# A two-layer streaming encoder on one core: decay tiles and attention tiles put in one ring of seven, a fifth key tile, and a planner reseeded every 16 jobs

## The chip, the core and the metric

The kernel runs on one core of a Trainium2 chip. Five engines work side by side and meet at semaphores: TensorE (PE in the rows of the profile, and PEld for its weight loads), VectorE (DVE), ScalarE (ACT), GpSimd (POOL) and SyncE (SP), which issues every DMA of this kernel. The metric is the device time of one execution in microseconds (us), as the median of repeated runs.

## The reference

The input is one sequence of 2048 frames of width 1024, and two layers act on it. Each computes `x + gate * Mixer(RMSNorm(x) * (1 + scale) + shift)`, where shift, scale and gate are linear in SiLU of a conditioning vector. The first mixer is a gated linear recurrence (RG-LRU). The second is gated DeltaNet with 8 heads of width 128, and the change is made there. For a chunk of frames with summed log-decays `g` it computes

```
decay_mask = exp(where(causal, g[i] - g[j], -inf))
a_mat = where(strict, (k_beta @ k.T) * decay_mask, 0)
t_mat = inverse(a_mat + I)
attn  = where(causal, (q @ k.T) * decay_mask, 0)
v_new = u - w @ state;   o = q_dec @ state + attn @ v_new
state = state * e_last + k_dec.T @ v_new
```

The state is handed from chunk to chunk, so this part is a chain. A final RMSNorm ends the program. All of it is in float32.

## The kernel before

The frames are cut into two units of 1024 (`u`), each into two tiles of 512 (`i`). Layer 1 makes x and z panels of its input projection (`in1`, jobs of 24 matmuls of 128x512, L711), convolves, gates and scans them, and multiplies by its output weights (`out1`). Layer 2 does the same with panels k, v, q and z of each head (`in2`), runs the delta rule per head, and multiplies by its output weights (`out2`). Every projection is three matmuls for a float32 product: high by high, high by low, low by high.

In layer 2 a job's result goes through a convolution (`xe`, `xf`: ACT L1021, then three taps on DVE, L763) and SiLU on ACT (L1028) and becomes `kt`, `qt` or `vt`. For every head and tile of 512 frames, `key_thread` takes a decay tile `ec`: a DMA brings the log-decays, POOL masks them, ACT takes exp of four 128x128 parts (L1139), DVE scales them (L1172). It transposes `kt` on PE (`pk`, L1146) into the token-major keys `kd`, squares these (L1157), and makes `ac`, the strict matrix times decay (L1184). `norm_q_thread` writes the queries to DRAM, reloads them transposed (`pq`) and squares them on ACT (`junkq`, L1219). `query_thread` multiplies q by k on PE (`pqk`, L1268), and DVE multiplies that by `ec` into a tile of its own, `at` (L1273); then `ec` is given back. `inverses_thread` inverts 32x32 blocks on DVE (L1303, L1306). `levels_thread` builds the inverse of 128x128 from these (`px`, `pr`, with `tf` as working tile: L1338 to L1388). `recurrence_thread` runs eight steps per head and unit: `pp` on PE (L1421, L1422), `zt` on DVE (L1430), `py` on PE (L1438), `yt` on ACT (L1444), `pS` on PE (L1450, L1451), the state on DVE (L1463). `decay_thread` makes the decays of a unit from the projection `pab` (L1066), whose split weights (`wabh`, L1052) lie in a `tf` tile until the last `pab`.

ACT has one table of functions at a time. A row `ACT_TABLE_LOAD` stands where the function it needs next (SiLU, exp, sqrt) is in another table.

The order of the instructions on every engine is not written out. A planner, `Weave`, runs while the program is built: each thread is a generator that yields an engine and an assumed duration, a ring of tiles (`Slots`), or an event, and the planner starts next whatever can start first by its own clock; instructions are emitted in that order. So a ring's size, a wait or an assumed duration moves instructions everywhere. Assumed durations off PE are scattered by 1% with a seeded generator, so the seed is also an input to the order. `job()` runs one panel by one tile: 64 jobs in `in1`, 128 in `in2`, 32 in `out1` and 33 in `out2`.

Of the kernel before, what the change touches and what calls it, by code (L numbers as in the profile page):

```python
# [32 lines left out]
KTN, QTN = 6, 5  # L33
MARGIN = 1.0
# [6 lines left out]
SEED, SPREAD = 3, 0.01  # L41
# [34 lines left out]
class Weave:  # L76
    def __init__(self):
        self.free = dict.fromkeys(("pe", "act", "dve", "pool", "sp", "dma"), 0.0)
        self.held = {"dve2": [], "pool2": []}
        self.table = "exp"  # L80
        self.landed, self.through = [0.0] * 8, 0.0
        self.scatter = random.Random(SEED)
        self.threads = []
        self.now = 0.0

# [85 lines left out]
def trunk_kernel(ctx, tc, x, head, small, ada0, ada_w, ada_b, final_g, w1, gate_w, ow1, w2, wab, ow2, out):  # L171
# [44 lines left out]
    def part_of(tile_in, at, *shape):  # L216
# [27 lines left out]
        "xe": 2, "xf": 2, "kt": KTN, "qt": QTN, "vt": 1, "ec": 3, "gr": 1, "middle": 1, "ac": 4, "atn": 4, "kd": 4, "vn": 4,  # L244
        "rq": 4, "nk": 4, "oo": 2, "tblk": 1, "ttmp": 1, "tf": 2, "zt": 2, "t2": 2, "yt": 2, "so": 2, "ro": 2,
# [3 lines left out]
    for t in ("xe", "xf", "vt", "ec", "gr", "middle", "ab", "gin", "gg", "spe", "spd"):  # L249
        tags[t] = ("l2a", tags[t][1])  # L250
    tags |= {"g2": ("o2a", 1), "fg": ("o2a", 1), "xta": ("o2a", 2)}
    tags |= {"oh": ("o2", 3), "ol": ("o2", 3), "xt": ("o2", 4), "ot": ("o2", 2)}
    slots = {t: Slots(n) for t, (_, n) in tags.items()}
    slots["turn"] = Slots(TURN)
    pools.update(xp=xp, ps=ps)
# [487 lines left out]
    def project_thread():  # L743
        for name, panels, jobs in plans:
            if name == ("out1",):
                yield from out1_jobs()
                continue
            for n in range(len(jobs)):
                if name == ("in1", 0) and n < 4:

                    w.spawn(job(name, jobs, n), 8 + n)
                    if n == 3:
                        for m in range(4):
                            yield ev("job", name, m)
                else:
                    yield from job(name, jobs, n)
        yield from out2_jobs()
# [199 lines left out]
    def out1_jobs():  # L957
        nb = S // P
        jobs = [(b + q, d) for b in range(0, nb, 2) for d in range(2) for q in range(2)]
        for b, d in jobs:  # L960
            yh, yl, htok, ltok = yield ev("yhl", b)
            ow = yield ev("owtiles", 1, d)
            bank = "d" if d else "mm"
            mtok = yield slots[bank]
            pt = ps.tile([P, TC], F32, tag=bank, name="mmo")
            yield from products(pt, (yh, yl), ow, (lambda k: ev("ow", 1, d, k // 2 * 2)))
            if d == 1:
                put("yh", htok)
                put("yl", ltok)
            w.spawn(residual1_thread(b, d, pt, bank, mtok), 3, 0.2)  # L970
            if b == nb - 1:
                w.set(ev("free", "out1", d))
# [152 lines left out]
    def key_thread(u, h, i):  # L1125
# [5 lines left out]
        ec = tile_([P, TB, P], "ec", "ec")  # L1131
# [129 lines left out]
    def query_thread(u, h, i):  # L1261
# [8 lines left out]
        xtok = yield slots["atn"]  # L1270
        yield "dve", 0.61
        at = tile_([P, TB, P], "atn", "at")
        dve.tensor_tensor(at, pqk, ec, ALU.mult)  # L1273
        put("tp", ptok)
        put("ec", etok)
        vn, ntk = yield ev("vn", u, h, i)
        toks = {"kt": ktok, "qt": qtok, "ac": atok, "atn": xtok, "kd": dtok, "vn": ntk}
        w.set(ev("parts", u, h, i), (kt, qt, ac, at, kd, vn, toks))
# [117 lines left out]
    def recurrence_thread(u, h):  # L1396
# [4 lines left out]
        for i in range(NTC):  # L1401
# [7 lines left out]
            for b in range(TB):  # L1409
# [45 lines left out]
                if b == TB - 1:  # L1455
                    release(toks, "ac", "vn", "kd", "atn")
# [81 lines left out]
    def queries_end_thread():  # L1538
        for i in range(NTC):
            yield ev("parts", NU - 1, NH - 1, i)  # L1540
            yield ev("rq", NU - 1, NH - 1, i)
        early.close()
# [60 lines left out]
    def out2_jobs():  # L1603
# [4 lines left out]
        for b, q in jobs:  # L1608
            c0, n = parts[b][q]
# [29 lines left out]
    def finish_thread(b, parts):  # L1639
        xt, tag, tok = yield ev("xt", b)  # L1640
        otag = "raw" if b < AHEAD else "ot"
        otok = yield slots[otag]
# [9 lines left out]
        for q in range(1, parts):  # L1652
# [4 lines left out]
        yield "pool", 1.34  # L1657
        rs = tile_([P, 1], "rs", "rs")
        rsqrt(rs, ss[:, 0:1], 1.0 / D, 1)
# [136 lines left out]
```

## Time and profile before

| what | value |
|---|---|
| median of the runs | 1860.39 us (3 runs, 1857.08 to 1862.02) |
| the profiled execution's own time | 1852.99 us |
| its span, first to last instruction | 1851.3 us |
| PE busy | 1798.8 us, 97% of the span |
| DVE, ACT, POOL busy | 1344.0, 1167.0, 358.4 us (73%, 63%, 19%) |
| layer 1 with its output | about 0 to 645 us |
| layer 2, unit 0 and unit 1 | about 645 to 1160 and 1160 to 1690 us |
| second output and final norm | about 1690 to 1851 us |

A row of waits reads: engine and the first instruction after the wait, then what ended the wait, then us in total, how often, and the longest. A row of a timeline reads: start, duration, engine, line, operation, output and inputs, how many, and in brackets the idle time of the engine before it and what ended it. A row of the chain of waits has start, duration and what the chain went through. Matmul ends are modelled, so a busy PE is not a PE at its best rate.

### The profile page before, as it was taken

Reading aid. Unit: us, or ns where it says so; the run is one execution under the profiler, and the core shown is the slowest. Engines: PE = TensorE matmul, PEld = TensorE weight load, DVE = VectorE, ACT = ScalarE, POOL = GpSimd, SP = SyncE. Lnnn points to the kernel's source line nnn. Section 1 sums busy time; section 2 is a strip of 40 time slices with the busy share of each in tenths; the row PEclk is TensorE's granted clock in tenths of the full one; section 3 lists DMA queues with packets and bytes.
Section 4 is the critical chain, followed back from the end, with each engine's and each line's share of the span. In section 5 each row is a group of like instructions: output and inputs, shape, how many; then the busy total and the mean of one; then the engine's idle time right before and its main releaser. Section 6 shows DMA issues by size and latency. Waiting matters only on the chain.

```text
span 1851.3 us, 31018 instructions
## 1 busy us (share of the span) xinstructions
PE 1798.8 (97%) x10270; PEld 1441.3 (78%) x10270; DVE 1344.0 (73%) x3112; ACT 1167.0 (63%) x2709; POOL 358.4 (19%) x896
## 2 busy tenths in 40 slices
PE   6999999999999999999999999999999999999998
PEld 4777777777878877787888787787788877778886
DVE  7989887877455647777888878577776687776653
ACT  5766777666111467786888766777778678654221
POOL 2111001010000013232323221232223223211100
PEclk9999999999999999999999999999999999999999
DMA  9577655545588645567677666366655556687741
GB/s 357 146 205 210 238 190 179 184 156 165 191 217 222 188 126 141 142 167 182 165 165 195 155 162 191 106 162 151 150 141 138 145 142 162 151 224 208 245 144 67
DMA packets 510425, 322.75 MB, mean 174 GB/s; under 512 B 369844, under 2 KB 437940, under 8 KB 510264
## 3 DMA queue, kind: packets, MB, share of 16 engines
q1 hardware_dynamic: 510264, 320.77, 62.0%
q8 instruction: 81, 1.33, 0.3%
q14 instruction: 80, 0.66, 0.1%
HBM read 219.93 MB, written 100.73 MB: 173 GB/s over the span
## 4 chain that ended last, share of the span: by engine, by line
PE 71%; DVE 9%; DMA 7%; ACT 7%; SPq 4%; issue 2%; POOL 1%; DVEq 0%; POOLq 0%; ACTq 0%
PE mm L711 39%; PE mmo L711 18%; PE pg L843 3%; DVE xf L763 2%; DMA raw<-in_w 2%; PE py L1438 1%; PE pp L1421 1%; PE pS L1450 1%; PE pS L1451 1%; PE pp L1422 1%; DVE ttmp L1303 1%; DVE tblk L1306 1%; DMA blk<-blk_d 1%; PE pqk L1268 1%; PE pkk L1180 1%
## 5 line engine op out<-in xcount | busy, mean ns | idle before, releaser
L763 DVE SCALAR_TENSOR_TENSOR xf<-xe,small_s,xf 128x512 f32<-128x512 f32 x288 | 214.1, 749 | 40.8 <-ACT xf L1021 37.2
L687 ACT CAST whi<-raw 128x1024 fp32r<-128x1024 f32 x96 | 100.0, 1042 | 50.1 <-DMA raw<-in_w 43.7
L1303 DVE TENSOR_TENSOR ttmp<-blk,tblk 128x60 f32<-128x60 f32 (+24 forms) x496 | 105.5, 213 | 17.3 <-DMA blk<-blk_d 5.7
L1306 DVE TENSOR_TENSOR tblk<-tblk,ttmp 128x60 f32<-128x60 f32 (+24 forms) x496 | 107.4, 217 | 12.2
L711 PE MATMUL mm<-hh_('in2', 0)_5148,whi 128*128 128x512 f32 x256 | 103.9, 406 | 2.2 <-DVE tf L1350 2.2
L711 PE MATMUL mm<-hh_('in2', 1)_11583,whi 128*128 128x512 f32 x256 | 104.5, 408 | 0.7 <-ACT tz L1036 0.7
L711 PE MATMUL mm<-hh_('in2', 0)_5148,wlo 128*128 128x512 f32 x256 | 104.2, 407 | 0.0
L711 PE MATMUL mm<-hh_('in2', 1)_11803,wlo 128*128 128x512 f32 x256 | 104.1, 407 | 0.0
L711 PE MATMUL mm<-hl_('in2', 1)_11584,whi 128*128 128x512 f32 x256 | 104.0, 406 | 0.0
L711 PE MATMUL mm<-hh_('in2', 1)_11583,wlo 128*128 128x512 f32 x256 | 104.0, 406 | 0.0
L711 PE MATMUL mm<-hl_('in2', 0)_5149,whi 128*128 128x512 f32 x256 | 103.8, 406 | 0.0
L711 PE MATMUL mm<-hl_('in2', 0)_5034,whi 128*128 128x512 f32 x256 | 103.6, 405 | 0.0
L711 PE MATMUL mm<-hl_('in2', 1)_11804,whi 128*128 128x512 f32 x256 | 103.5, 404 | 0.0
L711 PE MATMUL mm<-hh_('in2', 1)_11803,whi 128*128 128x512 f32 x256 | 103.5, 404 | 0.0
L711 PE MATMUL mm<-hh_('in2', 0)_5033,wlo 128*128 128x512 f32 x256 | 103.1, 403 | 0.0
L711 PE MATMUL mmo<-oh,oh 128*128 128x512 f32 (+1 forms) x264 | 102.8, 389 | 0.0
L711 PE MATMUL mmo<-ol,oh 128*128 128x512 f32 (+1 forms) x264 | 102.7, 389 | 0.0
L711 PE MATMUL mm<-hh_('in2', 0)_5033,whi 128*128 128x512 f32 x256 | 102.5, 400 | 0.0
L711 PE MATMUL mmo<-oh,ol 128*128 128x512 f32 (+1 forms) x264 | 102.4, 388 | 0.0
L711 PE MATMUL mmo<-oh,yl 128*128 128x512 f32 x256 | 100.5, 393 | 0.5 <-DVE yl L953 0.5
L711 PE MATMUL mmo<-oh,yh 128*128 128x512 f32 x256 | 100.8, 394 | 0.0
L711 PE MATMUL mmo<-ol,yh 128*128 128x512 f32 x256 | 100.8, 394 | 0.0
(317 smaller groups left out, 5322.0 us busy)
## 6 DMA issues: line engine op xcount, KB each, us to landing
raw<-in_w SPq DMA_DIRECT2D x96, 512.0 KB, 4.2
araw<-in_ada_w SPq DMA_DIRECT2D x32, 512.0 KB, 4.3
xt<-x_d SPq DMA_DIRECT2D x32, 512.0 KB, 5.4
xt_d<-xb SPq DMA_DIRECT2D x192, 64.0 KB, 2.7
xk<-xt_d SPq DMA_DIRECT2D x24, 512.0 KB, 5.7
xt<-in_x SPq DMA_DIRECT2D x16, 512.0 KB, 6.0
ada<-in_ada SPq DMA_DIRECT2D x16, 512.0 KB, 10.4
y_d<-tz SPq DMA_DIRECT2D x32, 256.0 KB, 3.0
```

The costliest lines, as they stand in the source:

```text
L687: act.copy(hi, raw)
L711: pe.matmul(pt, lhsT=lhs[a][:, k, :], rhs=rhs[b][:, k, :], start=(k == 0 and n == 0), stop=(k == KT - 1 and n == 2))
L763: dve.scalar_tensor_tensor(xf, xe[:, 1 + j:1 + j + TC], wc[:, j:j + 1], xf, ALU.mult, ALU.add)
L843: pe.matmul(pg, lhsT=gw[:, g, :], rhs=xf, start=True, stop=True)
L1180: pe.matmul(pkk[:, b, :], lhsT=kc, rhs=kc, start=True, stop=True)
L1268: pe.matmul(pqk[:, b, :], lhsT=kt[:, b * P:(b + 1) * P], rhs=qt[:, b * P:(b + 1) * P], start=True, stop=True)
L1303: dve.tensor_tensor(tmp, blk[:, j, j + 1:32].unsqueeze(2).to_broadcast([P, r, c_]), t[:, j, 0:c_].unsqueeze(1).to_broadcast([P, r, c_]), A ...
L1306: dve.tensor_tensor(t[:, j + 1:32, 0:c_], t[:, j + 1:32, 0:c_], tmp, ALU.subtract)
L1421: pe.matmul(pp[:, 0, :], lhsT=kc, rhs=S_, start=True, stop=True)
L1422: pe.matmul(pp[:, 1, :], lhsT=qc, rhs=S_, start=True, stop=True)
L1438: pe.matmul(py, lhsT=rm[:, b, :], rhs=zt, start=True, stop=True)
L1450: pe.matmul(pS[:, 0, :], lhsT=kd[:, b, :], rhs=yt, start=True, stop=True)
```

## The change

Seven tiles replace three of `ec` and four of `at`: `query_thread` now writes attention over the decays, in place, and the tile is given back when the recurrence has used it. Of the seven, three lie in the part of memory that is closed before the end of layer 2, four in the other; `queries_end_thread` waits for the three. `kd` has five tiles, not four, and `tf` one, not two. The planner's generator is seeded anew each 16 jobs, from a list of 17 seeds. In the last norm, `finish_thread` takes its output tile only after the second output weights were issued, and for the last block of frames it scales two parts of the sum of squares ahead, adds the third on DVE, and takes the power on POOL.

```diff
+EC = 7
-SEED, SPREAD = 3, 0.01
+SEEDS, SPREAD = (32, 45, 51, 36, 4, 54, 53, 16, 3, 25, 36, 8, 28, 14, 37, 0, 0), 0.01
...
+    def count(self):
+        self.jobs += 1
+        if self.jobs % 16 == 0:
+            self.scatter = random.Random(SEEDS[self.jobs // 16])
...
-        "xe": 2, "xf": 2, "kt": KTN, "qt": QTN, "vt": 1, "ec": 3, "gr": 1, "middle": 1, "ac": 4, "atn": 4, "kd": 4, "vn": 4,
-        "rq": 4, "nk": 4, "oo": 2, "tblk": 1, "ttmp": 1, "tf": 2, "zt": 2, "t2": 2, "yt": 2, "so": 2, "ro": 2,
+        "xe": 2, "xf": 2, "kt": KTN, "qt": QTN, "vt": 1, "ec": 4, "eca": 3, "gr": 1, "middle": 1, "ac": 4, "kd": 5, "vn": 4,
+        "rq": 4, "nk": 4, "oo": 2, "tblk": 1, "ttmp": 1, "tf": 1, "zt": 2, "t2": 2, "yt": 2, "so": 2, "ro": 2,
...
+    ECLAST = NU * NH * NTC - 1
+    slots["ec"] = Slots(EC)
...
-        ec = tile_([P, TB, P], "ec", "ec")
+        ec = tile_([P, TB, P], "eca" if (ECLAST - etok) % EC >= 4 else "ec", "ec")
...
-        xtok = yield slots["atn"]
         yield "dve", 0.61
-        at = tile_([P, TB, P], "atn", "at")
-        dve.tensor_tensor(at, pqk, ec, ALU.mult)
+        dve.tensor_tensor(ec, pqk, ec, ALU.mult)
         put("tp", ptok)
-        put("ec", etok)
...
-                    release(toks, "ac", "vn", "kd", "atn")
+                    release(toks, "ac", "vn", "kd", "ec")
+                    w.set(ev("ecfree", toks["ec"]))
...
+        for n in range(4, EC):
+            yield ev("ecfree", ECLAST - n)
...
+        if b < AHEAD:
+            yield ev("owissue", 2, 1)
...
-        for q in range(1, parts):
+        for q in range(1, 2):
...
-        yield "pool", 1.34
-        rsqrt(rs, ss[:, 0:1], 1.0 / D, 1)
+        if parts > 2:
+            yield "pool", 0.28
+            pool.tensor_scalar(ss[:, 0:1], ss[:, 0:1], 1.0 / D, EPS, ALU.mult, ALU.add)
+            yield ev("sq", b, 2)
+            yield "dve", 0.16
+            dve.scalar_tensor_tensor(ss[:, 0:1], ss[:, 2:3], 1.0 / D, ss[:, 0:1], ALU.mult, ALU.add)
+            yield "pool", 0.6
+            pool.tensor_tensor(rs, ss[:, 0:1], mhalf[:, 0:1], ALU.pow)
+        else:
+            yield "pool", 1.34
+            rsqrt(rs, ss[:, 0:1], 1.0 / D, 1)
```

The engines run nearly the same instructions as before: PE has 8350 matmuls in both, SP the same DMAs, DVE one instruction more and POOL one less (the last norm), and ACT has 97 table loads where it had 123. What differs besides is the order. Line numbers are up to 22 higher after the change, so L1038 there is L1028 here.

**First place**, ACT near the start of layer 2: the last `kt` row is the second key tile of head 1, and `junkq` squares the reloaded queries of head 0's second tile. Before:

```order
L775 COPY xe<-mm 128x512
L1157 ACTIVATE junk,ssk<-kd 128x128 x2
L1021 ACTIVATE xf<-xe,small_s 128x512
L1219 ACTIVATE junkq,ssq<-pq 128x128 x3
L1139 ACT_TABLE_LOAD
L1139 ACTIVATE ec<-ec,gc 128x128
L687 CAST whi<-raw_5931 128x1024
L1139 ACTIVATE ec<-ec,gc 128x128 x6
L1219 ACTIVATE junkq,ssq<-pq 128x128
L1139 ACTIVATE ec<-ec,gc 128x128
L1028 ACT_TABLE_LOAD
L1028 ACTIVATE kt<-xf 128x512
```

The same place now:

```order
L1031 ACTIVATE xf<-xe,small_s 128x512
L1167 ACTIVATE junk,ssk<-kd 128x128
L1038 ACTIVATE kt<-xf 128x512
L695 CAST whi<-raw_5935 128x1024
L1149 ACT_TABLE_LOAD
L1149 ACTIVATE ec<-ec,gc 128x128
L1160 COPY kd<-pk 128x512
```

The key tile comes ahead of the exps and both table loads, and `junkq` of that tile follows ten rows behind the last row shown.

**Second place**, DVE, the levels of head 2 in unit 0: `tf<-ac` transposes blocks for the matmuls `px`, and `tf<-px` takes their result back, for `pr` on PE. `tb<-qt` is the transpose of a query tile on its way to DRAM. Before:

```order
L763 SCALAR_TENSOR_TENSOR xf<-xe,small_s,xf 128x512 x6
L1338 STREAM_TRANSPOSE tf<-ac 32x4x32 x2
L1273 TENSOR_TENSOR at<-pqk,ec 128x512
L1338 STREAM_TRANSPOSE tf<-ac 32x4x32 x4
L1234 STREAM_TRANSPOSE tb<-qt 128x512
L693 TENSOR_TENSOR wlo<-raw_7954,whi 128x1024
L1350 TENSOR_SCALAR tf<-px 32x8x32
```

The same place now:

```order
L1345 STREAM_TRANSPOSE tf<-ac 32x4x32
L701 TENSOR_TENSOR wlo<-raw_7838,whi 128x1024
L1345 STREAM_TRANSPOSE tf<-ac 32x4x32
L772 SCALAR_TENSOR_TENSOR xf<-xe,small_s,xf 128x512 x3
L1357 TENSOR_SCALAR tf<-px 32x8x32
L507 TENSOR_SCALAR xt<-xt,rs 128x1024
L1244 STREAM_TRANSPOSE tb<-vt 128x512
```

Three taps stand between the last transpose and `tf<-px`, where a transpose to DRAM and a weight split stood.

**Third place**, DVE where unit 1 begins: `beta` is made from the last `pab`, and the `tf` rows are the levels of head 7 of unit 0. Before:

```order
L1350 TENSOR_SCALAR tf<-px 32x8x32
L613 TENSOR_TENSOR hl_('in2', 1)_11804<-h,hh_('in2', 1)_11803 128x512
L763 SCALAR_TENSOR_TENSOR xf<-xe,small_s,xf 128x512 x2
L1366 COPY ac<-pr 32x4x32
L763 SCALAR_TENSOR_TENSOR xf<-xe,small_s,xf 128x512
L1366 COPY ac<-pr 32x4x32 x2
L1234 STREAM_TRANSPOSE tb<-vt 128x512
L1376 TENSOR_SCALAR tf<-px_12148 64x256
L1385 COPY ac<-pr_12173 64x4x64
L1461 COPY state_106<-pS 128x128
L1471 COPY oo<-pS 128x128
L1087 TENSOR_SCALAR beta<-beta 128x64
```

The same place now:

```order
L1345 STREAM_TRANSPOSE tf<-ac 32x4x32 x4
L1097 TENSOR_SCALAR beta<-beta 128x64
L1345 STREAM_TRANSPOSE tf<-ac 32x4x32
L1101 TENSOR_TENSOR gin<-ab,small_s 128x64
L295 TENSOR_SCALAR gg<-gin 128x64
```

The levels of head 7 were done before `beta`; they begin now only when the last `pab` has let go of the one `tf` tile.

More of the change, by code (lines that the diff above doesn't have):

```diff
@@ L81, in __init__ @@
         self.landed, self.through = [0.0] * 8, 0.0
-        self.scatter = random.Random(SEED)
+        self.scatter, self.jobs = random.Random(SEEDS[0]), 0
         self.threads = []
         self.now = 0.0
+    def count(self):
+        self.jobs += 1
+        if self.jobs % 16 == 0:
+            self.scatter = random.Random(SEEDS[self.jobs // 16])
     def spawn(self, gen, prio, delay=0.0):
@@ L243, in trunk_kernel @@
     tags |= {t: ("l2", n) for t, n in {
-        "xe": 2, "xf": 2, "kt": KTN, "qt": QTN, "vt": 1, "ec": 3, "gr": 1, "middle": 1, "ac": 4, "atn": 4, "kd": 4, "vn": 4,
-        "rq": 4, "nk": 4, "oo": 2, "tblk": 1, "ttmp": 1, "tf": 2, "zt": 2, "t2": 2, "yt": 2, "so": 2, "ro": 2,
+        "xe": 2, "xf": 2, "kt": KTN, "qt": QTN, "vt": 1, "ec": 4, "eca": 3, "gr": 1, "middle": 1, "ac": 4, "kd": 5, "vn": 4,
+        "rq": 4, "nk": 4, "oo": 2, "tblk": 1, "ttmp": 1, "tf": 1, "zt": 2, "t2": 2, "yt": 2, "so": 2, "ro": 2,
         "ssk": 2, "ssq": 2, "rk": 2, "cc": 2, "junk": 1, "ab": 1, "gin": 1, "gg": 1, "spe": 1, "spd": 1, "beta": 2,
         "gs": 2, "eg": 2}.items()}
-    for t in ("xe", "xf", "vt", "ec", "gr", "middle", "ab", "gin", "gg", "spe", "spd"):
+    for t in ("xe", "xf", "vt", "eca", "gr", "middle", "ab", "gin", "gg", "spe", "spd"):
         tags[t] = ("l2a", tags[t][1])
@@ L748, in project_thread @@
             for n in range(len(jobs)):
+                w.count()
                 if name == ("in1", 0) and n < 4:
@@ L960, in out1_jobs @@
         for b, d in jobs:
+            w.count()
             yh, yl, htok, ltok = yield ev("yhl", b)
@@ L1269, in query_thread @@
                       start=True, stop=True)
-        xtok = yield slots["atn"]
         yield "dve", 0.61
-        at = tile_([P, TB, P], "atn", "at")
-        dve.tensor_tensor(at, pqk, ec, ALU.mult)
+        dve.tensor_tensor(ec, pqk, ec, ALU.mult)
         put("tp", ptok)
-        put("ec", etok)
         vn, ntk = yield ev("vn", u, h, i)
-        toks = {"kt": ktok, "qt": qtok, "ac": atok, "atn": xtok, "kd": dtok, "vn": ntk}
-        w.set(ev("parts", u, h, i), (kt, qt, ac, at, kd, vn, toks))
+        toks = {"kt": ktok, "qt": qtok, "ac": atok, "ec": etok, "kd": dtok, "vn": ntk}
+        w.set(ev("parts", u, h, i), (kt, qt, ac, ec, kd, vn, toks))
     def inverses_thread(u, h):
@@ L1608, in out2_jobs @@
         for b, q in jobs:
+            w.count()
             c0, n = parts[b][q]
```

## The prediction

> **What bounds the kernel now.** I read the page's busy line first, then the stretches, the waits of PE, and the chain of waits.
>
> ```profile
> PE 1798.8 (97%) x10270; PEld 1441.3 (78%) x10270; DVE 1344.0 (73%) x3112; ACT 1167.0 (63%) x2709; POOL 358.4 (19%) x896
> 0.00:645.00 645.00, 626.45 (x2689) 485.41 (x2690) 482.85 (x819) 355.63 (x486) 71.21 (x132) 1.00 0.66 204
> 645.00:1160.00 515.00, 501.05 (x3343) 406.96 (x3343) 398.47 (x1106) 381.16 (x1043) 136.92 (x362) 0.99 0.64 161
> 1160.00:1690.00 530.00, 517.70 (x3545) 422.44 (x3544) 376.30 (x1088) 392.37 (x1097) 133.14 (x353) 1.00 0.60 154
> ```
>
> The first row is the page's, the others are stretches (start and end, length, then busy time and count of PE, PEld, DVE, ACT, POOL, granted clock, DMA share and rate). PE bounds the kernel in every stretch, at a granted clock of 0.99 to 1.00. The change leaves PE's 8350 matmuls as they were, so it can gain only where PE stands still: 515.00 - 501.05 + 530.00 - 517.70 = 26.3 us idle in layer 2, plus weight loads that come late. ACT is busy for 381.16 of 515 us there, so it bounds nothing on the average; it matters by what it makes late. PE's waits, with those of its weight loads below (in total, how often, longest):
>
> ```profile
> PE pk L1146 <- ACT kt L1028: 4.2, 4, 3.1
> PE pS L1450 <- ACT yt L1444: 3.8, 5, 1.4
> PE mm L711 <- DVE tf L1350: 2.2, 1, 2.2
> PE py L1438 <- DVE zt L1430: 1.9, 2, 1.4
> PE pp L1421 <- DVE state L1463: 1.8, 3, 0.8
> ...
> PEld py L1438 <- DVE zt L1430: 13.7, 57, 1.9
> PEld pp L1421 <- DVE state L1463: 11.6, 47, 1.3
> PEld pS L1450 <- ACT yt L1444: 9.6, 20, 1.9
> ```
>
> Two single waits stand out, 3.1 us for a key tile and 2.2 us for `tf`. The rest is spread over many short ones, most of them at the recurrence.
>
> **First term, the key tile: -3.0 us.** ACT and PE around the longest wait:
>
> ```profile
> 706.12 0.71 ACT L1021 ACTIVATE xf<-xe,small_s 128x512 f32<-128x512 f32 x1
> 711.27 0.31 ACT L1219 ACTIVATE junkq<-pq 128x128 bf16<-128x128 f32 x1 [4.45 <-DMA pq<-q_d]
> 712.57 1.28 ACT L1139 ACT_TABLE_LOAD   x1
> 713.86 0.40 ACT L1139 ACTIVATE ec<-ec,gc 128x128 f32<-128x128 f32 x1
> 717.57 1.28 ACT L1028 ACT_TABLE_LOAD   x1
> 718.86 0.63 ACT L1028 ACTIVATE kt<-xf 128x512 f32<-128x512 f32 x1
> 719.54 0.33 PE L1146 MATMUL pk<-ident,kt 128*128 128x128 f32 x1 [3.05 <-ACT kt L1028]
> ```
>
> ACT stands for 4.45 us before `junkq`, whose reload is late, then changes tables, runs exps, changes back, and only then makes `kt`. In the new order (first place above) this `kt` comes ahead of the exps, both loads and `junkq`. So I take the whole 3.05 us as gone. If the reload is late again, what stands behind `junkq` now is exps and `kd` rows of head 1, which PE needs only for that head's levels and recurrence, after DVE has inverted its blocks. I cost that at nothing; without this cover the 3 us come back. Bounds: 0 (another row takes its part) to -3.3 (with a late weight load, an estimate).
>
> **Second term, `tf` of head 2: -2.2 us.**
>
> ```profile
> 863.83 0.71 DVE L1234 STREAM_TRANSPOSE tb<-qt 128x512 f32<-128x512 f32 x1 [3.76 <-DMA v_d<-tb]
> 864.46 1.21 DVE L693 TENSOR_TENSOR wlo<-raw,whi 128x1024 fp32r<-128x1024 f32 x1
> 865.70 0.43 DVE L1350 TENSOR_SCALAR tf<-px 32x256 f32<-32x256 f32 x1
> 866.18 0.50 PE L711 MATMUL mm<-hh_('in2', 0)_5148,whi 128*128 128x512 f32 x1 [2.22 <-DVE tf L1350]
> ```
>
> DVE stands for 3.76 us before `tb<-qt`, since a DMA has not yet emptied the tile it writes; behind it wait a weight split and `tf<-px`, and behind that PE. Now three taps stand in that place (second place above), 3 x 0.75 us, that hang on no DMA just before. I counted all 16 levels in the orders: between the last transpose and `tf<-px` stood 13 transposes to DRAM and weight splits, and now 7. So the pattern is rarer, not only gone here. Bounds 0 to -2.2.
>
> **Third term, the table loads: -3.8 us.** The page's groups and the first and last of the table loads on the chain of waits of layer 2:
>
> ```profile
> L1139 ACT ACT_TABLE_LOAD x29 | 37.2, 1283 | 0.5
> L1028 ACT ACT_TABLE_LOAD x24 | 30.8, 1283 | 0.4
> L1036 ACT ACT_TABLE_LOAD x8 | 10.3, 1283 | 1.1 <-PE mm L711 0.9
> ...
> 689.74 1.28 ACT L1139
> 691.74 1.28 ACT L1028
> ...
> 1509.54 1.28 ACT L1139
> ```
>
> Layer 2 had 29 + 24 + 8 = 61 loads for exp, SiLU of k, q, v, and SiLU of z; in the new order it has 18 + 20 + 1 = 39. That frees ACT of 22 x 1.283 = 28.2 us, which is not a gain in itself: ACT is not the bound. What counts is the loads on the chain that ended last. Nine of the 61 lie there; two of these belong to the first term. The two shown at 689.74 and 691.74 stand around one exp between SiLU rows, and the new order has neither there: 2 x 1.28 = 2.6 us. Of the other five, two lie in the same first stretch and stay. For the last three I take the share of loads that falls away elsewhere: from the first `qt` to the first `kt` of head 2 the loads go from 10 to 4, so elsewhere from 51 to 35, 31%; 0.31 x 3 x 1.28 = 1.2. Together -3.8. Bounds: 0, if other work of ACT fills the time, and 7 x 1.28 = -9.0. In layer 1 the loads go from 59 to 55, and none was on the chain: 0.
>
> The Trainium skill ("ScalarE: Activation LUTs", What ACT_TABLE_LOAD costs) gives the same 1283 ns, and adds a drain of about 1380 ns, 2.66 us for each switch. The trace does not show the drain: after the load at 712.57 the exp starts at 713.86, and idle time before 29 loads sums to 0.5 us. By the skill's figure the third term would be 2.07 times as large.
>
> **Fourth term, shorter cover at the recurrence: +2.6 us.** In a chain step PE needs other work to hide `zt`, `yt` and the state. I summed, in both orders, the PE work between `pp` and `py`, `py` and `pS`, `pS` and the next `pp`, by 0.23 us for a long matmul and 0.11 for a short one. Steps with under 0.6 us of it: 6, 5 and 8 before; 14, 9 and 9 now: 13 more. A short step's price lies between 0.02 (the 7.5 us of idle PE in the three rows above, over 367 steps) and 0.39 (the same over the 19 short steps alone). I take the middle, 0.2: 13 x 0.2 = 2.6. Bounds +0.3 and +5.1.
>
> **Fifth term, the tail: -0.3 us.**
>
> ```profile
> 1844.86 0.19 ACT L1636 ACTIVATION_READ_ACCUMULATOR ot<-xt 128x1 f32 x1
> 1845.18 0.19 POOL L1655 TENSOR_TENSOR ss<-ss 128x1 f32<-128x1 f32 x1 [2.62 <-ACT ot L1636]
> 1845.46 0.19 POOL L281 TENSOR_SCALAR ss<-ss 128x1 f32<-128x1 f32 x1
> 1845.74 0.55 POOL L282 TENSOR_TENSOR rs<-ss,mhalf 128x1 f32<-128x1 f32 x1
> ```
>
> Three POOL steps follow the last partial sum, 0.28 us apart; the change leaves two steps, one on DVE, so one step goes. A slower hand-over from DVE to POOL would bring it to 0.
>
> **Edits at nothing.** The multiply in place is the same DVE instruction and waits for the same matmul:
>
> ```profile
> DVE at L1273 <- PE pqk L1268: 15.8, 16, 4.0
> ```
>
> It could now wait for ACT too, which reads a column of `ec` for `kd`; those rows already stand ahead of `pqk` by the thread's own order. Seven shared tiles hold what 3 + 4 held, and the fifth `kd` only lets a key tile start sooner. The wait for the second output weights is met long before: their last issue is at 1666.37, the first output's at 1683.86.
>
> ```profile
> 1666.37 0.43 SPq L920 DMA_DIRECT2D oraw<-in_ow  x1
> ...
> 1683.86 0.43 SPq L1674 DMA_DIRECT2D out<-ot  x1
> ```
>
> The start of the program stands in the same order on every engine for its first 34 rows; its idle time (most of the first stretch's 18.6 us) stays. One `tf` tile is costed at nothing with its cover named below.
>
> **The sum.** -3.0 - 2.2 - 3.8 + 2.6 - 0.3 = -6.7 us. The profiled execution took 1852.99 us, so it would be 1846.3. The median of the runs before, 1860.39, lies 7.4 us higher; with the same -6.7 it becomes **1853.7**.
>
> **Rivals.** *The waits are only drawn anew.* The whole order moved, and a late DMA that stood before `kt` may now stand before another row. Then the first two terms come back, +5.2: 1858.9, no change that can be told. For it: both waits began with a DMA that landed late, and DMAs are as many. Against it: the counts of 61 to 39 loads and 13 to 7 rows.
>
> *One `tf` tile makes head 7 late (slower).* The third place. In the trace:
>
> ```profile
> 1126.99 0.28 DVE L1054 TENSOR_TENSOR wabh<-wabr,wabh 128x128 fp32r<-128x128 f32 x1
> 1150.17 0.48 DVE L1338 STREAM_TRANSPOSE tf<-ac 32x128 f32<-32x128 f32 x2
> 1162.11 0.40 PE L1066 MATMUL pab<-hl_('in2', 1)_11804,wabh 128*32 128x512 f32 x1
> 1164.98 0.49 PE L1438 MATMUL py<-vn,ac 128*128 128x128 f32 x2
> ```
>
> The decay weights held one `tf` from 1127 to 1162.5, while the levels of head 7 used the other from 1150.2. With one tile they start at 1162.5, 12.3 us later, and `py` at about 1177. If PE had nothing for these 12.3 us, the result would be 1853.7 + 12.3 = 1866.0, slower. Against it: the new order puts 24 us of PE work between the last `pab` and that recurrence, projections of unit 1. It makes the kernel slower from 6.7 us of uncovered wait on, and by over 0.3% only if all 12.3 lie open.
>
> *The short steps cost far more.* At 1.9 us each, the longest wait in the rows above, 13 of them make +24.7 in place of +2.6: 1875.8. It is slower from (6.7 + 2.6 + 5.6) / 13 = 1.15 us a step on; only the longest waits are so long.
>
> *Table switches cost more than their rows show.* If ACT also ran empty for as long as a load before each switch, the third term would double to -7.6: 1849.9. Against it: the 0.5 us of idle time before 29 loads. The Trainium skill's section named above ("ScalarE: Activation LUTs", What ACT_TABLE_LOAD costs) speaks for it.
>
> **How the numbers follow.** 0.3%, 5.6 us, is about what a measurement of this kernel can tell from no change. Chances: the forecast 0.49, and the dearer switches 0.05, both faster; the waits drawn anew 0.28, the same; one `tf` 0.09 and dear short steps 0.09, slower. So faster 0.54, same 0.28, slower 0.18. The forecast's own range, with the third and fourth terms at their bounds, is 1846.2 (-5.2 and -2.3 further) to 1860.0 (+3.8 and +2.5). The low end of the range, 1842, leaves 4 us below that for other waits among the 26.3 us of idle time. The high end, 1865, takes in the waits drawn anew and most of the late `tf`.
>
> **What would show it.** Right: ACT's table loads 97 x 1.28 us; no wait of `pk` over 1 us near 720; no wait of PE for `tf<-px` over 1 us; PE idle in layer 2 near 20 us, where it was 26.3. The fourth term shows in the PE and PEld waits of the recurrence, some 2 to 5 us more in total. The tail shows one POOL step less. Wrong: new single waits over 2 us behind a DMA, or PE without matmuls between the last `pab` and head 7.

## The result, and the profile after

The changed kernel takes 1840.18 us, the median of 4 runs (1838.72 to 1841.39), beside 1861.2 for 4 runs of the kernel before: a ratio of 0.9889, 95% interval 0.9869 to 0.9909. It is 21 us faster, three times the forecast gain of 6.7, and below the range. With more runs the gain is smaller: in the repeat of the experiments the two take 1840.3 (4 runs) and 1855.7 (24 runs), 15.4 us apart, a ratio of 0.9918 (0.9899 to 0.9937). That is still more than twice the forecast gain. The profiled execution took 1839.34 us with a span of 1837.2, against 1852.99 and 1851.3 before, so this pair differs by 14.1 us of span. Where 14 and 21 come from is taken up below, under what a wait of PE costs.

The busy line of the changed kernel's page:

```profile
PE 1796.2 (98%) x10270; PEld 1442.9 (79%) x10270; DVE 1343.3 (73%) x3113; ACT 1136.8 (62%) x2683; POOL 359.9 (20%) x895
```

Its stretches, in the columns used before:

```profile
0.00:645.00 645.00, 627.22 (x2683) 485.59 (x2684) 480.61 (x818) 349.39 (x480) 69.54 (x130) 1.00 0.66 204
645.00:1160.00 515.00, 505.38 (x3309) 412.15 (x3308) 400.13 (x1107) 372.86 (x1038) 141.38 (x366) 1.00 0.65 162
1160.00:1690.00 530.00, 523.14 (x3650) 429.47 (x3649) 384.02 (x1098) 383.17 (x1100) 134.81 (x359) 1.00 0.61 158
```

PE stands still for 515.00 - 505.38 + 530.00 - 523.14 = 16.5 us in layer 2, where it was 26.3. Over the whole span, idle PE falls from 1851.3 - 1798.8 = 52.5 to 1837.2 - 1796.2 = 41.0. Busy PE falls by 2.6 with the same number of matmuls, so it also runs a little faster. 11.5 + 2.6 is the 14.1 of this pair.

PE's waits, with those of its weight loads, in the changed kernel:

```profile
PE px L1379 <- DVE ac L1373: 2.7, 2, 1.5
PE pp L1428 <- DVE state L1471: 2.6, 3, 1.0
...
PE pr L1364 <- ACT tf L1355: 1.5, 1, 1.5
...
PE pS L1457 <- ACT yt L1451: 1.2, 4, 0.4
...
PE py L1445 <- DVE zt L1437: 0.5, 1, 0.5
...
PEld pp L1428 <- DVE state L1471: 11.4, 41, 1.4
PEld py L1445 <- DVE zt L1437: 10.6, 48, 0.9
PEld pS L1457 <- ACT yt L1451: 6.0, 15, 0.8
```

Neither `pk <- kt` (3.1) nor `mm <- tf` (2.2) is left, and PE's longest wait in layer 2 is now 1.5 us. One wait of 1.5 us is new, `pr` for a `tf<-px` that ACT makes, so the sign "no wait of PE for `tf<-px` over 1 us" does not hold everywhere. ACT at the place of the first term:

```profile
710.77 0.64 ACT L1038 ACTIVATE kt<-xf 128x512 f32<-128x512 f32 x1 [2.10 <-DVE xf L772]
...
712.35 1.28 ACT L1149 ACT_TABLE_LOAD   x1
713.65 0.40 ACT L1149 ACTIVATE ec<-ec,gc 128x128 f32<-128x128 f32 x1
...
717.07 0.30 ACT L1229 ACTIVATE junkq<-pq 128x128 bf16<-128x128 f32 x1
```

`kt` comes ahead of the table load, the exps and `junkq`, as the order said, 8 us earlier than in the profile before. The tail's last sum:

```profile
1831.76 0.19 ACT L1647 ACTIVATION_READ_ACCUMULATOR ot<-xt 128x1 f32 x1
1832.05 0.16 DVE L1676 SCALAR_TENSOR_TENSOR ss<-ss 128x1 f32<-128x1 f32 x1 [0.65 <-ACT ot L1647]
1832.30 0.55 POOL L1678 TENSOR_TENSOR rs<-ss,mhalf 128x1 f32<-128x1 f32 x1 [2.56 <-DVE ss L1676]
```

The power starts 0.35 us after the last partial sum; it was 0.69.

So the two named waits and the tail went nearly as the prediction said, and its sum was still far too small. The experiments ask which part of the change carries the gain, and why.

### The profile page after: what moved, and what is told of

Same layout as the page of the kernel before. It is cut to its first block, busy times and chain, and to the rows that moved or that the text cites. A ratio compares the mean times of both kernels' runs of the same rounds, so it can differ in the third digit from the quotient of the medians.

```text
span 1837.2 us, 31008 instructions
## 1 busy us (share of the span) xinstructions
PE 1796.2 (98%) x10270; PEld 1442.9 (79%) x10270; DVE 1343.3 (73%) x3113; ACT 1136.8 (62%) x2683; POOL 359.9 (20%) x895
## 4 chain that ended last, share of the span: by engine, by line
PE 70%; DVE 9%; DMA 8%; ACT 5%; issue 3%; SPq 3%; POOL 1%; DVEq 0%; POOLq 0%; ACTq 0%
PE mm L719 39%; PE mmo L719 17%; PE pg L852 3%; DVE xf L772 2%; DMA raw<-in_w 1%; PE py L1445 1%; PE pp L1428 1%; PE pS L1457 1%; PE pS L1458 1%; PE pp L1429 1%; DVE tblk L1313 1%; PE pqk L1278 1%; DVE ttmp L1310 1%; PE pkk L1190 1%; DMA blk<-blk_d 1%
## 5 line engine op out<-in xcount | busy, mean ns | idle before, releaser
L719 PE MATMUL mm<-hh_('in2', 1)_11863,whi 128*128 128x512 f32 x256 | 104.0, 406 | 0.7 <-ACT tz L1046 0.7
L719 PE MATMUL mm<-hh_('in2', 1)_11588,whi 128*128 128x512 f32 x256 | 104.3, 408 | 0.1
L719 PE MATMUL mm<-hl_('in2', 1)_11864,whi 128*128 128x512 f32 x256 | 104.0, 406 | 0.0
L719 PE MATMUL mm<-hh_('in2', 0)_5144,whi 128*128 128x512 f32 x256 | 103.7, 405 | 0.0
L719 PE MATMUL mm<-hh_('in2', 1)_11588,wlo 128*128 128x512 f32 x256 | 103.7, 405 | 0.0
L719 PE MATMUL mm<-hl_('in2', 1)_11589,whi 128*128 128x512 f32 x256 | 103.5, 404 | 0.0
L719 PE MATMUL mm<-hh_('in2', 1)_11863,wlo 128*128 128x512 f32 x256 | 103.4, 404 | 0.0
L719 PE MATMUL mm<-hh_('in2', 0)_5144,wlo 128*128 128x512 f32 x256 | 103.2, 403 | 0.0
L719 PE MATMUL mm<-hl_('in2', 0)_5145,whi 128*128 128x512 f32 x256 | 102.8, 402 | 0.0
## 6 DMA issues: line engine op xcount, KB each, us to landing
ada<-in_ada SPq DMA_DIRECT2D x16, 512.0 KB, 10.4
```

The lines of the kernel that those rows point to most:

```text
L719: pe.matmul(pt, lhsT=lhs[a][:, k, :], rhs=rhs[b][:, k, :], start=(k == 0 and n == 0), stop=(k == KT - 1 and n == 2))
```

## Experiments

| kernel | median, us | ratio to before, 95% | idle PE, us | half clock, us | table loads | ACT and DVE wait for DMA in layer 2, us |
|---|---|---|---|---|---|---|
| before, first profile | | | 52.5 | 6.8 | 123 | 69.8 |
| before, again | 1857.1 | 0.9984 to 1.0011 | 53.9 | 23.9 | 123 | 69.9 |
| reseeding alone | 1863.8 | 1.0034 to 1.0061 | 56.0 | 30.7 | 123 | 66.2 |
| changed, one seed | 1858.1 | 1.0005 to 1.0026 | 56.2 | 23.9 | 97 | 70.7 |
| changed, again | 1840.3 | 0.9899 to 0.9937 | 41.2 | 3.4 | 97 | 41.9 |
| before with tanh | 1851.2 | 0.9950 to 0.9985 | 49.2 | 13.7 | 61 | 76.2 |
| changed with tanh | 1834.5 | 0.9841 to 0.9918 | 38.6 | 3.4 | 57 | 49.0 |
| changed, second list | 1850.6 | 0.9951 to 0.9988 | 50.0 | 10.2 | 97 | 65.5 |
| changed, third list | 1853.0 | 0.9976 to 1.0001 | 50.0 | 10.2 | 101 | 46.8 |
| before, second list | 1854.3 | 0.9977 to 1.0002 | 47.7 | 17.1 | 127 | 67.3 |
| before, third list | 1887.0 | 1.0146 to 1.0192 | 73.6 | 47.8 | 133 | 64.0 |
| before, two waits gone | 1854.5 | 0.9982 to 1.0013 | 51.0 | 13.7 | 123 | 59.3 |
| changed, copy eightfold | 1866.7 | 1.0048 to 1.0084 | 60.2 | 13.7 | 97 | 37.9 |
| changed, copy fourfold | 1848.1 | 0.9932 to 0.9970 | 49.0 | 6.8 | 97 | 45.8 |
| before, short loads | 1838.0 | 0.9880 to 0.9920 | 40.8 | 0 | 123 | 36.8 |
| changed, short loads | 1832.3 | 0.9842 to 0.9887 | 36.6 | 0 | 97 | 25.5 |
| changed, two `tf`, four `kd` | 1863.6 | 1.0023 to 1.0054 | 55.5 | 41.0 | 95 | 56.9 |
| before, early loads | 1858.1 | 1.0002 to 1.0022 | 53.1 | 27.3 | 135 | 64.4 |
| changed, early loads | 1856.0 | 0.9995 to 1.0020 | 50.6 | 10.2 | 99 | 37.8 |

Idle PE is the span less PE's busy time in the profiled execution. Half clock is the time in which the clock's records show 0.5, after the first 60 us and without the last stretch, which ends the program. The last column sums the waits of ACT and DVE that a DMA ended, from 645 to 1700 us. Medians and ratios are those of all runs of a row, the other columns those of its one profiled execution. The runs were made on five chips, on which the kernel before took 1855.4 to 1857.2 us, so rows of different chips compare to within about 2 us. The two tanh kernels, the two with short loads and the one with two waits gone leave work out, as their texts say.

### Which part carries the gain: tiles or seeds

The kernel before, unchanged:

> The kernel before, unchanged, to have a second trace of it. Theory A (the profiled execution of before was a low one: it lay 8 us under the median, while that of the change lay 1 us under its own): 1857 to 1864 us, ratio 1.000, and this trace shows some 5 to 8 us more of PE waits in layer 2 than the first, at places where a DMA lands late. Theory B (the two differ in what lies outside the span): the same waits as in the first trace, and the surplus outside the span.

The kernel before with the list of seeds alone (the change's counter of jobs, `count`, goes in with it and is not shown):

```diff
-SEED, SPREAD = 3, 0.01
+SEEDS, SPREAD = (32, 45, 51, 36, 4, 54, 53, 16, 3, 25, 36, 8, 28, 14, 37, 0, 0), 0.01
...
```

> The kernel before with the generator seeded anew each 16 jobs by the same list, tiles and last norm as before. Theory R (the ring of seven makes the gain): the order is merely drawn anew, within 5 us of before; ACT has 123 table loads as before. Theory S (the list of seeds makes the gain): at least 8 us faster than before.

The changed kernel, its last norm too, with the one seed of before:

```diff
-        self.scatter, self.jobs = random.Random(SEEDS[0]), 0
+        self.scatter, self.jobs = random.Random(3), 0
...
-        if self.jobs % 16 == 0:
-            self.scatter = random.Random(SEEDS[self.jobs // 16])
```

> The change with its ring of seven, five key tiles, one tf tile and the new last norm, but one seed (3) throughout as before. Theory R (ring): 97 table loads are there with one seed already, so most of the 21 us stays, 12 to 20 us faster than before. Theory S (seeds): the list fits its planner's order, and without it at most 8 us are left.

The changed kernel again:

> The change itself on the same chip as the three others: 1.1% faster than before again, 1838 to 1842 us if before is 1857 to 1864. It is the measure for the parts.

Measured: 1857.1, 1863.8, 1858.1 and 1840.3. The seeds alone lose 0.5% and the tiles alone (with the new last norm) gain nothing, so neither has the gain by itself. The reseeded kernel, 8 us slower, fits neither R nor S; the one with one seed goes against R and fits S. Theory A was right that the first profile was a low one, but not why: the second has only 1.4 us more idle PE, and 9.0 us more busy PE. The kernel with one seed has the table loads of the changed one, 97, and two single waits that neither kernel of the change has:

```profile
PE pr L1362 <- ACT tz L1044: 4.6, 1, 4.6
PE pr L1362 <- ACT xe L782: 4.1, 1, 4.1
```

Two lists drawn at random were then put in the changed kernel and in the kernel before (the second list in the changed kernel is shown).

```diff
-SEEDS, SPREAD = (32, 45, 51, 36, 4, 54, 53, 16, 3, 25, 36, 8, 28, 14, 37, 0, 0), 0.01
+SEEDS, SPREAD = (1595, 1867, 1199, 1930, 1988, 1552, 1946, 1367, 1478, 1049, 1679, 1515, 1219, 1616, 1227, 1939, 1295), 0.01
```

> The changed kernel with seventeen other seeds, drawn at random, in place of the seventeen of the change; tiles, reseeding each 16 jobs and everything else as in the change. Theory F (the list was fitted to this kernel's planner, and the gain is that of a chosen draw): no gain, 1850 to 1865. Theory M (the move to new seeds at each 16 jobs, together with the new tiles, is what helps, whatever the seeds): 1838 to 1846.

> The changed kernel with a third list of seventeen seeds drawn at random, beside the second list, which took 1850.6 where the list of the change took 1840. Theory F (the change's list is a chosen draw; without the choice the new tiles land between 1850 and 1860): 1848 to 1862. Theory M (reseeding with the new tiles helps whatever the seeds, and the second list was an unlucky one): 1838 to 1846.

> The kernel before with its own tiles, reseeded each 16 jobs from the second list. With the changed tiles this list took 1850.6. Theory K (the tiles have a worth of their own, whatever the draw): 5 us or more above that, 1856 to 1866. Theory Z (the tiles alone are worth nothing, and each pair of tiles and list is a draw of its own): as likely below 1850.6 as above, somewhere from 1845 to 1866; the two kernels of each list then differ with either sign.

> The kernel before with its own tiles, reseeded each 16 jobs from the third list. Theory K: 5 us or more above the changed kernel with the same list. Theory Z: with either sign, within 15 us.

Measured: with the changed tiles 1850.6 and 1853.0, with the tiles of before 1854.3 and 1887.0. Theory M falls, and F holds: the new tiles with other lists take 10 to 13 us more. Of K and Z neither is settled: the second list misses K's 5 us, and the third Z's 15. Changed less before tiles is +1 to +2 us with the one seed, -23.5 with the change's list, -3.7 and -34 with the others. The tiles may be worth something on the average, but four pairs with such a spread don't give a number. The draw of the order alone moves the kernel from 1840 to 1858 with the changed tiles and from 1854 to 1887 with those of before, over four lists each.

The worst draw shows what a bad order does. Its longest wait of PE, and ACT in it:

```profile
PE px L1352 <- ACT tz L1043: 14.9, 1, 14.9
```

```profile
1133.59 1.28 ACT L1264 ACTIVATE vn<-vn,nk 128x128 f32<-128x128 f32 x4 [8.66 <-DMA vn<-v_d]
```

ACT stands for 8.66 us before a reload that has not landed, and stands again before other late reloads behind it; the `tz` that PE waits for comes only at 1147.32.

Last, two tile counts of the change were put back, with its list kept:

```diff
-        "xe": 2, "xf": 2, "kt": KTN, "qt": QTN, "vt": 1, "ec": 4, "eca": 3, "gr": 1, "middle": 1, "ac": 4, "kd": 5, "vn": 4,
-        "rq": 4, "nk": 4, "oo": 2, "tblk": 1, "ttmp": 1, "tf": 1, "zt": 2, "t2": 2, "yt": 2, "so": 2, "ro": 2,
+        "xe": 2, "xf": 2, "kt": KTN, "qt": QTN, "vt": 1, "ec": 4, "eca": 3, "gr": 1, "middle": 1, "ac": 4, "kd": 4, "vn": 4,
+        "rq": 4, "nk": 4, "oo": 2, "tblk": 1, "ttmp": 1, "tf": 2, "zt": 2, "t2": 2, "yt": 2, "so": 2, "ro": 2,
```

> The changed kernel with two tf tiles and four kd tiles, as before the change, and all else as changed, its list of seeds too. The order moves from the first place where a tile count decides. Theory F (the list fits the tiles it was chosen with): the gain goes, 1848 to 1862. Theory Q (the list, or the seven shared tiles with the multiply in place, carry the gain by themselves): it stays, 1836 to 1844. The rival of the prediction that one tf tile makes head 7 late would show as a gain of up to 12 us here.

Measured 1863.6: the gain is gone, as F expects, though 1.6 us above its range. The rival that one `tf` tile makes head 7 late would have shown as a gain, and none is seen; the order moved as well. Of the combinations run here, only this list with just these tiles has the gain.

### Table loads

In both kernels the SiLU of the second layer was replaced by a tanh, with the order kept; the result is no longer the layer's.

```diff
-        act.activation(r, xf, AF.Silu)
+        act.activation(r, xf, AF.Tanh)
```

> The kernel before with its SiLU of q, k, v and z in the second layer replaced by a tanh, which shares its table with the exponentials: 61 table loads in place of 123, every instruction in the same order on its engine. It leaves out the SiLU of these four, so that the values differ from the reference; the work is otherwise the same. Theory L (the third term of the prediction: table loads end waits of the chain, and the change gained by having fewer of them): 62 loads fewer at a gain of at least 0.4 us each for those on the chain, 9 to 11 of them, so 4 us or more, and up to 25 us if the other loads count too: 1830 to 1852. Theory D (the gain is in the draw of the order, not in the loads): at most the few microseconds of the loads that stand on the chain, 1850 to 1858, and the long waits of TensorE stay where they were.

> The changed kernel with the same replacement (its second layer's SiLU of q, k, v and z left out for a tanh): 57 table loads in place of 97, the order unchanged. With four loads between it and the kernel before with the tanh, theory L expects the two within 3 us of each other, since the cause of the difference is gone. Theory D expects the difference between the two kernels with the tanh to be as large as between the two without, 12 to 20 us, and this kernel at 1833 to 1841.

Measured 1851.2 and 1834.5, beside 1855.4 for the kernel before on that chip. 62 loads fewer are worth 4.2 us in the kernel before, 0.07 us each; 40 fewer in the changed kernel are worth 5.8 (1840.3 less 1834.5, from two chips), 0.15 each. The first run fits L and D alike; the second decides. With nearly equal loads, 61 and 57, the two kernels still differ by 16.7 us. D holds; the loads are not the cause. The Trainium skill ("ScalarE: Activation LUTs", What ACT_TABLE_LOAD costs) adds a drain of about 1380 ns to each switch. No trace here shows it: with 62 switches fewer ACT's busy time falls by 79 us, which is 62 x 1.28, and the idle time before 29 loads was 0.5 us in the prediction's row.

### The two named waits

In the kernel before, order kept, the two causes were taken away; `plain` is true for unit 0, head 3, first half.

```diff
+            src = qt[:, b * P:(b + 1) * P] if (u, h, i) == (0, 0, 1) else pq[:, b, :]
-            act.activation(junk, pq[:, b, :], AF.Square, accum_out=ss[:, b:b + 1])
+            act.activation(junk, src, AF.Square, accum_out=ss[:, b:b + 1])
...
-        dve.transpose(out=tb, in_=ap.rearrange("p (a i) -> p a i", i=32))
+        if not plain:
+            dve.transpose(out=tb, in_=ap.rearrange("p (a i) -> p a i", i=32))
```

> The kernel before, order unchanged, with what makes the prediction's two named waits taken away: the four squares of q at 711 us (unit 0, head 0, second half) read the query tile itself in place of the reload that lands late, and the query of head 3, first half, is stored as it lies, without the transpose into the tile that a store still holds (DVE has 0.71 us less to do there). It leaves out that transpose and takes the sum of squares over the wrong axis for these tiles, so values differ. Theory N (the two terms, -3.0 and -2.2, are worth what the prediction said): 5 us below the kernel before, 1848 to 1852, and no window of half clock after 866 us, which would give up to 1.7 us more. Theory T (another late row takes the place of each wait): 0 to -2 us, 1853 to 1858, with a wait of PE for another row of over 1.5 us near 719 or 866.

Measured 1854.5, a ratio of 0.9997 (0.9982 to 1.0013), which is -3.3 to +2.4 us: no change that can be told, where N expected 5 us. The two waits are still there, a little shorter:

```profile
PE pk L1146 <- ACT kt L1028: 3.3, 4, 2.1
PE mm L711 <- DVE tf L1353: 1.7, 1, 1.7
```

ACT ahead of `kt` in this kernel, and DVE ahead of `tf<-px`:

```profile
706.87 1.28 ACT L1139 ACT_TABLE_LOAD   x1
710.08 0.40 ACT L1139 ACTIVATE ec<-ec,gc 128x128 f32<-128x128 f32 x1 [1.93 <-POOL ec L1135]
712.09 1.05 ACT L687 CAST whi<-raw 128x1024 fp32r<-128x1024 f32 x1 [1.60 <-DMA raw<-in_w]
...
716.80 0.63 ACT L1028 ACTIVATE kt<-xf 128x512 f32<-128x512 f32 x1
```

```profile
863.22 1.23 DVE L693 TENSOR_TENSOR wlo<-raw,whi 128x1024 fp32r<-128x1024 f32 x1 [3.80 <-ACT whi L687]
864.48 0.43 DVE L1353 TENSOR_SCALAR tf<-px 32x256 f32<-32x256 f32 x1
```

Without the late `junkq`, ACT waits 1.93 us for POOL and 1.60 for a weight panel; without the late transpose, DVE waits 3.80 us for the split of a panel. These were hidden behind the rows that came last. T holds, though the rows that took over stand in the same place, not elsewhere.

### What a wait of PE costs

The prediction priced a wait at its length. The clock in the trace shows more. Four stretches of the kernel before in its second profile; the last three columns are granted clock, DMA share and rate:

```profile
868.20:871.60 3.40, 1.14 (x6) 0.86 (x5) 2.35 (x4) 3.33 (x7) 0.61 (x2) 1.00 1.12 283
871.70:878.50 6.80, 6.67 (x75) 4.90 (x74) 5.81 (x18) 3.29 (x6) 1.78 (x8) 0.50 0.97 261
987.80:991.20 3.40, 3.40 (x52) 2.85 (x53) 1.57 (x4) 3.30 (x10) 2.44 (x7) 0.50 1.11 330
1673.90:1677.30 3.40, 3.40 (x12) 2.85 (x11) 1.79 (x4) 0.74 (x2) 0.00 (x0) 0.50 0.83 223
```

PE worked for 1.14 of 3.40 us, and then ran at half clock for 6.8 us. A stretch of 3.41 us at half clock costs up to 1.7 us of PE's work. To test the price, waits were added in the changed kernel, by repeating a copy that PE waits for, at 8 of 16 inverses, eight times (shown) or four:

```diff
-        act.activation(tf[32:64, :, :, 0:32], px[32:64], AF.Copy, scale=-1.0)
+        for _ in range(8 if (u * NH + h) % 2 else 1):
+            act.activation(tf[32:64, :, :, 0:32], px[32:64], AF.Copy, scale=-1.0)
```

> The changed kernel, in which the copy of px into tf on ScalarE, 375 ns, is issued eight times in place of once for every other of the 16 inverses: 8 places at which TensorE's next products wait some 2.6 us longer, with the order unchanged. Theory P (a wait costs its own length): the span grows by what the rows of TensorE's waits grow, at most 8 x 2.6 = 21 us, and the granted clock stays at 1.00 between the waits. Theory C (TensorE's clock is halved for 3.41 us or a multiple of it after some of its long waits, as in the stretches at 868 and 1045 us of the kernel before): the span grows by more than the waits, by 1.7 us for each window of 3.41 us at half clock, of which there are then several between the first and the last of the eight places, 5 to 30 us beyond the sum of the waits.

> The changed kernel with the copy of px into tf issued four times in place of eight at every other inverse: 1.1 us late in place of 2.6. Theory C (a window of 3.41 us in which TensorE stands for more than about 1 us is followed by one at half clock): few waits are long enough, so 0 to 2 such stretches where the eightfold copy had four, and the time lies under 8 x 1.1 = 9 us above the changed kernel, 1841 to 1850. Theory G (any added wait is answered by a stretch at half clock): 4 or more such stretches and 10 us or more, above 1850.

Measured 1866.7 and 1848.1. With eight copies the span is 27.3 us longer than the changed kernel's: 19.2 of idle PE (60.2 - 41.0) and 8.1 of longer busy time (1804.3 - 1796.2), with four stretches at half clock (13.7 us, up to 6.8 lost). One of them, with the wait ahead of it:

```profile
1305.40:1308.60 3.20, 1.27 (x6) 0.73 (x4) 2.06 (x4) 3.08 (x8) 1.50 (x2) 1.00 0.35 134
1308.80:1312.20 3.40, 2.99 (x9) 2.57 (x10) 1.14 (x2) 3.19 (x7) 1.00 (x4) 0.51 0.02 5
```

Three of the four stretches begin within 6 us of an eightfold copy; the one at 926.6 us comes 14 us behind one, after another wait of 1.5 us. C holds, near its lower end, and P falls. With four copies the time is some 8 us up and there are two such stretches. Neither stands behind a lengthened copy: one, at 276.5 us, is in layer 1, and the other, at 1106.0, follows a wait of 2.1 us at an inverse with its single copy. So none of the eight shorter waits was answered by half clock, and G falls.

This bears on the 14 and the 21. In the first profile the kernel before ran at half clock for 6.8 us after the first 60 us, in the second for 23.9. The waits are nearly the same (52.5 and 53.9 idle), yet PE is busy for 1798.8 in the one and 1807.8 in the other, and the spans differ by 10.4. The first execution happened to run less at half clock. Against the second, the changed kernel has 12.9 us less idle time and 11.6 less busy time; but that execution, 1863.37 us, is the longest of its ten. The other executions have a granted clock and no trace. The 106 of the kernel before beside the experiments have a mean span of 1857.4 us where the clock was 0.993 (10 of them) and 1851.6 where it was 0.997 (22). At an equal clock, 0.996, they have 1853.6 (24), and two executions of the changed kernel have 1839.3 and 1840.2. So about 14 us of the gain do not hang on the clock, about as much as the first pair shows; the 21 rests on four runs of before that were long beside the others.

### Late transfers

The named waits and the longest of the third list began with a late transfer. In the second layer each weight panel was therefore cut from 512 to 64 KB, with the order kept; seven eighths of these weights are left out.

```diff
-        sp.dma_start(out=raw, in_=(w1 if layer == 1 else w2)[n])
+        if layer == 1:
+            sp.dma_start(out=raw, in_=w1[n])
+        else:
+            sp.dma_start(out=raw[:, 0:1, :], in_=w2[n][:, 0:1, :])
+            raw = raw[:, 0:1, :].to_broadcast([P, KT, P])
```

> The kernel before, order unchanged, whose 64 weight panels of the second layer load 64 KB in place of 512 KB each; the cast repeats that eighth over the panel, so seven eighths of these weights are left out. Theory W (TensorE's long waits of the second layer begin with weight panels and reloads that land late): the waits of ScalarE for weight loads, 25 to 29 us there, fall below 8, TensorE's idle time falls by 8 us or more, and the time by 10 us or more, to 1845 or less. Theory E (the waits come from the order of the work on ScalarE and VectorE; a load that comes sooner only shows the next late row, as with the two named waits): at most 5 us less, 1850 to 1858.

> The changed kernel with the same short weight loads (seven eighths of the second layer's weights left out). Theory W: little to gain, since its order leaves fewer such waits: 0 to 5 us less, 1835 to 1841, and the difference to the kernel before with short loads shrinks below 8 us. Theory E: the difference stays 12 to 22 us.

Measured 1838.0 and 1832.3. The kernel before gains 19 us and comes down to the time of the change, with the same idle PE (40.8) and no half clock. The changed kernel gains 8, more than W allowed, and the difference shrinks to 5.7, from 15.4 in the repeat. W holds in the main. ACT's waits for weight panels in layer 2, in the kernel before, the changed kernel, and the kernel before with short loads:

```profile
ACT whi L687 <- DMA raw<-in_w: 25.1, 16, 4.6
```

```profile
ACT whi L695 <- DMA raw<-in_w: 20.7, 19, 2.9
```

```profile
ACT whi L691 <- DMA raw<-in_w: 6.7, 3, 2.3
```

The change did not take these waits away; it has 20.7 us of them, none over 2.9. All waits of ACT and DVE for DMA together fall from 69.8 to 39.8, and to 36.8 with short loads. The short loads also leave the queues freer for every other transfer. The first stretch of layer 2, before with short loads, moves 134 GB/s (last column) where it was 161, and PE idles for 9.9 us where it was 13.95:

```profile
645.00:1160.00 515.00, 505.08 (x3406) 410.17 (x3405) 400.55 (x1114) 383.49 (x1051) 136.60 (x362) 1.00 0.55 134
```

So the panels' own part is not separated.

Would loading each panel earlier do the same, with nothing left out?

```diff
+                if name[0] == "in2" and not ahead:
+                    ahead.append((yield from panel_load(name, p)))
                 htok = yield slots["whi"]
```

> The kernel before, in which each weight panel of the second layer is loaded one panel ahead, before the tiles of its two parts are free; nothing is left out, and the order is drawn anew. Theory W2 (the panels are late because they are issued late): ScalarE's waits for weight loads in the second layer fall from 25 us to below 8, and the time falls by 8 us or more, to 1848 or less. Theory X (the new order brings other late rows, as each new order has): 1850 to 1865, whatever these waits do.

> The changed kernel with the same early loads; its list of seeds was not chosen for this order. Theory W2: the waits for weight loads fall from 21 us to below 8, and the time is 1832 to 1842, so that the early load makes up for the lost fit of the list. Theory X: 1845 to 1862, as with the two other lists.

Measured 1858.1 and 1856.0. No wait of ACT for a weight panel is left in layer 2, yet nothing is gained; X holds. In the kernel before with early loads another transfer is late:

```profile
ACT tz L1038 <- DMA z_d<-tz: 14.6, 2, 9.7
```

The changed kernel with early loads has as few waits for DMA as the change, 37.8 us, and is 16 us slower. So transfers that land late make a large part of the idle time of the kernel before, as the short loads show, but the sum of the waits for them does not tell which order is fast: the changed kernel with the third list has 46.8 us of them and takes 1853.0, the kernel before with tanh 76.2 and 1851.2. No kernel here beats the changed one with all work done.

## Why the prediction was right or wrong

- **Direction: right, with luck in it.** Faster was its likeliest case. But the terms behind it brought no gain by themselves: with one seed the 97 loads gained nothing, and without the causes of the two named waits no gain can be told.
- **The steps that failed.** The median missed by 13.5 us: 7.0 in the profiled execution's time and 6.6 in the offset from there to the median. Of the 7.0, 5.8 is the fourth term: it was to add 2.6 us, and PE's own waits at the recurrence fell by 3.2. Another 2.6 is PE's busy time, which the sum took as unchanged. What is left, 1.4 the other way, is not put down to a row.
- **First and second term, -3.0 and -2.2.** The order was read rightly, and both waits are gone. What failed is the pricing of each at its full length. With their causes taken away and the order kept, the two waits lost 1.0 and 0.5 us and the time nothing. In the change they went with the whole order around them.
- **Third term, -3.8.** The count of 97 came out. The price stays open: the same 97 loads in the kernel with one seed gave nothing, while 26 loads at the 0.07 and 0.15 us measured with the tanh are 1.8 to 3.8 us (an estimate). Whether "loads on the chain" is what sets it is not shown. The rival of dearer switches, -7.6, is not borne out.
- **Fourth term, +2.6: wrong sign.** The recurrence's waits fell, those of PE from 7.5 to 4.3 us and those of PEld from 34.9 to 28.0. The steps with little PE work between were no measure of them, and what DVE and ACT were late by was not in the count. That they came sooner because they wait less for DMA (the table's last column) is likely, not shown.
- **Fifth term, -0.3: right,** 0.34 measured.
- **The rival "waits only drawn anew"** came nearest to the mechanism, with the wrong result. It was valued at the old time, as though a new draw could only give back the two terms. The eight pairs of tiles and list measured here run from 1840 to 1887, and the change's list, with its tiles, is the best of them. That a draw has a wide spread of its own was the term left out of the sum.
- **From the profiled time to the median: +7.4, wrong.** The sum gave 1846.3 for the profiled execution, which took 1839.34: 7.0 too high. The median then got the same 7.4 as before and missed by 13.5. For the changed kernel the offset is 0.8 us. That the 7.4 was time at half clock, as in the second profile, is likely; no trace of those runs shows it.
- **The rivals of one `tf` tile and of dear short steps** did not come about: PE's longest wait in layer 2 is 1.5 us, and those at the recurrence are at most 1.0.

What stays open is the cause that decides between orders: which property of this one keeps PE supplied where the others do not. It could not be read from the list of seeds, nor from a count of waits.

## What to carry to other kernels

A wait in the profile names the row that came last; before pricing it, look what the next row behind it waits for, since in the two places tried here only the gap between the two was to be had. A change that moves a planner's whole order is a draw: give its time a width from runs of other seeds, or from the idle time and the late transfers, and look for the shared cause (here the transfers of one layer, worth 19 us) rather than for single waits. Compare medians with care when one kernel's executions spread over 10 us and the other's over 3: four runs put the gain at 21 us and 24 runs of before at 15, and the granted clock of each execution helps to tell the two parts apart.

## What the runs showed of the hardware

The half-clock stretches were not expected. Within an execution they begin on a fixed grid: those shown above start at 871.7, 987.8 and 1673.9 us, 34 and 201 times 3.413 us apart. 17 profiled executions have 55 such stretches after the first 60 us, and each lasts 3.41 us or a multiple. Each time PE had stood still, by the modelled ends of its matmuls, for 1.07 to 3.41 us (median 1.83) of the 3.41 us just ahead. Idle time alone does not decide it: up to 1.84 us in one period also went unanswered, and what else counts is not shown. In the kernel before, a wait lies now in one period, now across two; that is a likely reason, not a shown one, why nearly the same idle time, 52.5 and 53.9 us, came with 10 us more span in one execution than in the other.

The Trainium skill ("TensorE: Matmul & The Clock Gate", Part 1: The HAM clock gate) says that the clock is set by a free-running window of 3413 ns, and the grid agrees. It also says that the half rate comes after an idle window of about 3.4 us; here 1.07 us of a window without work was enough in one case, so the measurement decides.
